# Before the attention, elementwise work of GpSimd moved to VectorE, with embedding preparation and inverse products queued elsewhere

## The chip, the cores and the metric

The kernel runs on one core of a Trainium2 chip. TensorE (PE) multiplies matrices, VectorE (DVE), ScalarE (ACT) and GpSimd (POOL) do elementwise work, SyncE (SP) starts most transfers. Each engine works through its own list of instructions in the order in which they were put there when the kernel was built; semaphores hold an instruction until its inputs are there. The metric is the device time of one execution, in microseconds; less is better.

## The reference, cut to what matters

One layer on 1024 tokens of width 1024, all in float32:

```
h    = layer_norm(x)
proj = h @ w_in                                   # 3600 columns
q,k,v = silu(causal_conv4(proj[:, :1536]))        # 4 delta-rule heads of 128
z     = proj[:, 1536:2048]
o_gdn = gated_delta_rule(q, k, v, beta, decay)    # by chunks: (I + A)^-1, then a scan over chunks
fq,fk,fv = proj[...]                              # 8 attention heads of 64
o_fox = rms_norm(forgetting_attention(fq, fk, fv))
h = layer_norm(ALPHA*h + concat(rms_norm(o_gdn)*silu(z), o_fox) @ w_out)
ff  = square(relu(h @ w_up)) @ w_down
ple = (p @ w_ple) * sigmoid(h @ w_ple_gate)
out = layer_norm(ALPHA*h + ff + ple)
```

## The kernel before, in words

Precision first: float32 operands of a big matmul are split into a rounded half (`_hi`, a ScalarE cast) and a remainder (`_lo`, the difference of the two, `split_lo`, L54), and three products are summed.

The work runs in stages.

1. **Start** (L226 to L330). `p` and `w_ple` are loaded; `ple_prep` (L275 to L278) transposes `p` on TensorE and splits it (`pth`, `ptl`); `ple_mm` (L286) makes 16 tiles of the embedding product and sends them to DRAM. The weights of the values, `wv`, are loaded in eight tiles and split. Then for each of the eight token tiles `ln_rows` normalises a row tile `h`, `to_act` transposes it into `act_hi`/`act_lo`, and 48 matmuls `psv` (L309) make the attention's values and the gates.
2. **Projections** (`proj_ch`, L216). A projection column is 128 outputs for all tokens: its weights are loaded and split by `load_w` (`in_raw`, `in_hi`, `in_lo`), then two halves of 24 matmuls fill one PSUM bank each, of three. `conv_silu` (tiles `g`, `cv`) follows for the 12 delta-rule columns; `fox_proj` (`fq`, `fk`) and `z_proj` (`gz`) make the 12 others.
3. **Delta-rule set work**, for a pair of heads at a time (`hp` 0 and 1). `gdn_a` makes the chunk matrices (`tm` decay, `qd`, `kd`, `ka`, `am`); `gdn_fs` inverts 32x32 blocks by 31 forward steps of two VectorE operations each (`ftmp`, `ft`), writes them to DRAM and reads them back as `tm` and `ttm`; `gdn_b` combines blocks to full inverses with matmuls (`ps_p`, `ps_tp`, `ps_ttp`); `gdn_chain` scans eight chunks (`ps_ks`, `ps_vn`, `ps_s`, `ps_o`).
4. **Attention** (`ps_sc`, `ps_pt`, `ps_av`), then the output projection (`ps_mix`), the MLP and the last norm. The diff leaves these as they are, but projections that are not done when the attention starts (`fq`, `fk`, `gz`) run between its matmuls; the last `gz` columns stand in one run in front of the last two attention heads.

The order on each engine is made when the kernel is built: a scheduler takes instructions by priority (`tc.cur_priority`, lower first) and by its own idea of when they are ready. `background` (L658) gives the `fq`, `fk` and `gz` columns a priority 20000 later than the rest, so that they fill TensorE where nothing else is ready. Nothing reorders the lists at run time.

## Time and profile before

| | |
|---|---|
| median of 3 runs | 1489.93 us (1484.91 to 1490.1) |
| the profiled execution | 1487.18 us, of which 1485.5 us from its first to its last instruction (the span) |
| busy time in the span | PE 1398.8, weight loads 1177.5, DVE 1084.3, ACT 561.6, POOL 249.4 us |
| instructions | 20635 |

All of POOL's busy time lies in the first 700 us, in which the stages 1 to 4 up to the output projection run. A busy PE means that at least one matmul was under way, by modelled ends; times of waits are those of the engine that stood idle, and the name behind an arrow is what ended the wait.

### The profile page before, as it was taken

Reading aid. Unit: us, or ns where it says so; the run is one execution under the profiler, and the core shown is the slowest. Engines: PE = TensorE matmul, PEld = TensorE weight load, DVE = VectorE, ACT = ScalarE, POOL = GpSimd, SP = SyncE. Lnnn points to the kernel's source line nnn. Section 1 sums busy time; section 2 is a strip of 40 time slices with the busy share of each in tenths; the row PEclk is TensorE's granted clock in tenths of the full one; section 3 lists DMA queues with packets and bytes.
Section 4 is the critical chain, followed back from the end, with each engine's and each line's share of the span. In section 5 each row is a group of like instructions: output and inputs, shape, how many; then the busy total and the mean of one; then the engine's idle time right before and its main releaser. Section 6 shows DMA issues by size and latency. Waiting matters only on the chain.

```text
span 1485.5 us, 20635 instructions
## 1 busy us (share of the span) xinstructions
PE 1398.8 (94%) x7342; PEld 1177.5 (79%) x7342; DVE 1084.3 (73%) x2222; ACT 561.6 (38%) x1024; POOL 249.4 (17%) x196
## 2 busy tenths in 40 slices
PE   4999999789899899989999999999999999999997
PEld 3888787777788787777888988888888888888885
DVE  6647799567567887274889877777777789657877
ACT  4432422232136676272113333333333444455431
POOL 4313351036106433442000000000000000000000
PEclk9999999999999999999999999999999999999999
DMA  6765432525534333523377674444444986334342
GB/s 222 254 187 170 158 100 78 160 84 161 149 107 140 99 97 95 160 86 114 135 240 221 184 245 148 154 150 148 147 141 147 327 299 211 98 99 126 109 140 80
DMA packets 196638, 229.11 MB, mean 154 GB/s; under 512 B 23877, under 2 KB 129590, under 8 KB 196534
## 3 DMA queue, kind: packets, MB, share of 16 engines
q1 hardware_dynamic: 187142, 221.48, 47.5%
q10 hardware_dynamic: 9008, 5.24, 1.4%
q8 instruction: 58, 0.95, 0.3%
q0 software_dynamic: 384, 1.06, 0.2%
q14 instruction: 46, 0.38, 0.1%
HBM read 152.14 MB, written 75.60 MB: 153 GB/s over the span
## 4 chain that ended last, share of the span: by engine, by line
PE 70%; DVE 14%; DMA 6%; issue 3%; ACT 2%; POOL 2%; SPq 0%; DVEq 0%; ACTq 0%; POOLq 0%
PE ps_uP L1186 21%; PE ps_da L1306 9%; PE ps_db L1306 9%; DVE cv L51 4%; PE ps_gP L1053 4%; PE ps_db L1412 3%; PE gz L216 3%; PE psv L309 3%; PE ps_mix L932 2%; PE ps_av L779 2%; DVE ft L48 2%; PE ps_pt L765 2%; DVE ftmp L48 2%; PE g L216 1%; PE fk L216 1%
## 5 line engine op out<-in xcount | busy, mean ns | idle before, releaser
L1186 PE MATMUL ps_uP<-T,uS 128*128 128x512 f32 x576 | 133.8, 390 | 0.0
L1186 PEld LDWEIGHTS ps_uP<-T,uS 128*128 128x128 f32 x576 | 108.1, 188 | 23.4
L1276 ACT CAST rh<-rr 128x512 fp32r<-128x512 f32 x112 | 69.8, 623 | 138.8 <-PE ps_da L1306 51.6
L54 DVE TENSOR_TENSOR rl<-rr,rh 128x512 fp32r<-128x512 f32 x112 | 76.9, 687 | 59.0 <-ACT rh L1276 24.8
L1186 PE MATMUL ps_uP<-B,uA 128*128 128x512 f32 x384 | 92.2, 395 | 0.0
L932 PE MATMUL ps_mix<-wo,act_hi 128*128 128x512 f32 x256 | 82.8, 398 | 3.8 <-POOL wo L54 1.7
L1186 PEld LDWEIGHTS ps_uP<-B,uA 128*128 128x128 f32 x384 | 72.0, 188 | 17.4
L216 PE MATMUL g<-act_hi,in_hi 128*128 128x512 f32 x192 | 75.9, 395 | 3.4 <-DVE cv L51 3.3
L54 POOL TENSOR_TENSOR in_lo<-in_raw,in_hi 128x1024 fp32r<-128x1024 f32 x24 | 58.9, 2454 | 114.9 <-ACT in_hi L190 114.9
L216 PE MATMUL g<-act_hi,in_lo 128*128 128x512 f32 x192 | 76.0, 396 | 0.0
L216 PE MATMUL g<-act_lo,in_hi 128*128 128x512 f32 x192 | 75.8, 395 | 0.0
L1276 ACT CAST rl<-B 128x512 fp32r<-128x512 f32 x96 | 59.6, 622 | 24.6 <-PE ps_db L1306 12.4
L1181 ACT CAST uS<-wS 128x512 fp32r<-128x512 f32 x64 | 39.5, 622 | 73.2 <-issue 48.2
L54 DVE TENSOR_TENSOR uA<-uraw,uA 128x512 fp32r<-128x512 f32 x48 | 33.1, 690 | 46.3 <-ACT uA L1181 46.3
L54 DVE TENSOR_TENSOR ql<-B,rl 128x512 fp32r<-128x512 f32 x96 | 65.6, 684 | 0.3
L51 DVE SCALAR_TENSOR_TENSOR cv<-g,hcw,cv 128x511 f32<-128x511 f32 (+2 forms) x72 | 53.2, 739 | 7.9 <-ACT cv L413 7.5
L932 PEld LDWEIGHTS ps_mix<-wo,act_hi 128*128 128x128 f32 x256 | 47.5, 189 | 14.3 <-POOL wo L54 2.4
L54 DVE TENSOR_TENSOR ptl<-ps_pt,pth 128x512 fp32r<-128x512 f32 (+2 forms) x96 | 51.0, 552 | 9.3 <-ACT pth L767 8.9
L743 ACT ACTIVATE s<-s,m 128x128 f32<-128x128 f32 (+3 forms) x64 | 49.9, 780 | 13.0 <-DVE m L740 12.7
L765 PE MATMUL ps_pt<-ident,s 128*128 128x128 f32 x288 | 45.6, 275 | 9.0 <-DVE szl L51 4.0
L767 ACT CAST pth<-ps_pt 128x512 fp32r<-128x512 f32 (+2 forms) x96 | 43.9, 477 | 19.9 <-PE ps_pt L765 18.6
L1306 PE MATMUL ps_db<-rl,rh 128*128 128x512 f32 x192 | 51.3, 389 | 0.0
(372 smaller groups left out, 3836.3 us busy)
## 6 DMA issues: line engine op xcount, KB each, us to landing
uraw<-in_w_up_dram SPq DMA_DIRECT2D x32, 512.0 KB, 4.5
B<-in_w_down_dram SPq DMA_DIRECT2D x32, 512.0 KB, 5.5
rr<-rS SPq DMA_DIRECT2D x64, 256.0 KB, 2.7
in_raw<-in_w_in_dram SPq DMA_DIRECT2D x24, 512.0 KB, 3.8
rr<-rA SPq DMA_DIRECT2D x48, 256.0 KB, 2.9
h_spill<-h SPq DMA_DIRECT2D x16, 512.0 KB, 4.0
qkr<-qk_spill SPq DMA_DIRECT2D x32, 256.0 KB, 4.2
rA<-ub SPq DMA_DIRECT2D x32, 256.0 KB, 2.2
```

What stands on the lines that cost most here:

```text
L48: eng.tensor_tensor(out=o, in0=a, in1=b, op=op)
L51: nc.vector.scalar_tensor_tensor(out=o, in0=a, scalar=s, in1=b, op0=op0, op1=op1)
L54: eng.tensor_tensor(out=lo, in0=src, in1=hi.bitcast(F32), op=ALU.subtract)
L216: nc.tensor.matmul(ps, w[:, k, :], a[n][:, :, k], start=(k == 0 and wi == 0), stop=(k == NK - 1 and wi == 2))
L309: nc.tensor.matmul(ps[:, 0:264], a[t // 4][:, t % 4, k], w[:, k, _sl(n, 264)], start=(k == 0 and wi == 0), stop=(k == NK - 1 and wi == 2))
L743: nc.scalar.activation(out=s[:, :W], in_=s[:, :W], func=AF.Exp, bias=m[:, i:i + 1], scale=-1.0, accum_out=pairs[h // 2][2][:, r, j:j + 1])
L765: nc.tensor.transpose(pt[:, i], s[:, _sl(k0 + i)], ident)
L932: nc.tensor.matmul(ps, a[t // 4][:, t % 4, k], w, start=(k == 0 and wi == 0), stop=(k == NK - 1 and wi == 2))
L1053: nc.tensor.matmul(ps[j // 2][:, j % 2], B[b][s][k][:, _sl(j)], a[w][:, k], start=(first and j % 2 == 0 and k == 0 and wi == 0), stop=(j % ...
L1186: nc.tensor.matmul(ps[p], w[:, k], B[t][b][k], start=(chain is None and k == 0 and wi == 0), stop=(k == 3 and wi == 2), skip_group_check=c ...
L1276: nc.scalar.copy(out=hi, in_=src)
L1306: nc.tensor.matmul(ps[j], rs[x][:, _sl(j)], qs[y], start=(not chain and c == 0 and wi == 0), stop=(c == NP - 1 and wi == 2), skip_group_ch ...
```

## The change

It has four parts.

- Tensor operations that stood on GpSimd now stand on VectorE: the remainders of `load_w` and of `wv` (24 of 128x1024 and 8 of 128x520), the four operations per pair on `tm`, the two each on `qd`, `am`, `ka`, `kd`, and half of the last product on `vb`. `ln_rows` of the first norm takes its VectorE form: one product of a subtraction for the whole row and one product with a sum for each half, in place of a ScalarE, a VectorE and a GpSimd operation.
- The embedding's rows are taken in another order (`(q t)` for `(t q)`), so that a partition reads four whole rows in one piece. The first `ple_prep` stands ahead of the small VectorE work of the start, the second one ahead of the second column half of the first four tiles.
- `issue_after(x)` puts a block's instructions behind instruction `x` on x's engine; it adds no wait. `gdn_b(0)` goes behind the first half of column `fq0` on TensorE, `gdn_b(1)` behind the first half of `fk2`, and the exponential of the second pair's `tm` behind the end of the first chain on ScalarE.
- Priorities: the remaining delta-rule columns 2000, the background 20000, the second pair 4000 later.

```diff
@@ load_w, load_wv
-        split_lo(nc.gpsimd, wl, raw, wh)
+        split_lo(nc.vector, wl, raw, wh)
...
-                split_lo(nc.gpsimd, wv_lo[:, k, 0:520], raw, wv_hi[:, k, 0:520])
+                split_lo(nc.vector, wv_lo[:, k, 0:520], raw, wv_hi[:, k, 0:520])
@@ start
-        pv = p.rearrange("(t q) c -> q t c", q=P)
+        pv = p.rearrange("(q t) c -> q t c", t=NT)
+        ple_rows = ple_spill.rearrange("(q t) c -> t q c", t=NT)
...
-            nc.sync.dma_start(out=ple_spill[_sl(t), _sl(n, 512)], in_=so)
-        for half in range(2):
-            ple_prep(half)
-            for n in range(2):
-                for t in range(half * 4, half * 4 + 4):
-                    ple_mm(t, n)
+            nc.sync.dma_start(out=ple_rows[t, :, _sl(n, 512)], in_=so)
+        prep0 = ple_prep(0)
+        with tc.issue_after(prep0):
+            nc.vector.tensor_copy(out=wv_hi[:, :, 520:528], in_=wvs)
+            split_lo(nc.vector, wv_lo[:, :, 520:528], wvs, wv_hi[:, :, 520:528])
+        for t in range(4):
+            ple_mm(t, 0)
+        ple_prep(1)
+        for t in range(4):
+            ple_mm(t, 1)
+        for n in range(2):
+            for t in range(4, 8):
+                ple_mm(t, n)
...
-            ln_rows(xts.pop(t), gb, bb, h, "spread")
+            with tc.issue_after(prep0) if t == 0 else ExitStack():
+                ln_rows(xts.pop(t), gb, bb, h)
@@ gdn_a
-            tt(nc.gpsimd, c["tm"], c["tm"], gam[:, h * 8:h * 8 + 8].unsqueeze(2).to_broadcast([P, 8, P]), ALU.subtract)
-            tt(nc.gpsimd, c["tm"], c["tm"], mask_d.unsqueeze(1).to_broadcast([P, 8, P]), ALU.add)
-            nc.scalar.activation(out=c["tm"], in_=c["tm"], func=AF.Exp)
-            tt(nc.gpsimd, c["qd"], c["ka"][:, 1], c["am"], ALU.mult)
+            tt(nc.vector, c["tm"], c["tm"], gam[:, h * 8:h * 8 + 8].unsqueeze(2).to_broadcast([P, 8, P]), ALU.subtract)
+            tt(nc.vector, c["tm"], c["tm"], mask_d.unsqueeze(1).to_broadcast([P, 8, P]), ALU.add)
+            with tc.issue_after(chain_end[0]) if hp else ExitStack():
+                nc.scalar.activation(out=c["tm"], in_=c["tm"], func=AF.Exp)
+            tt(nc.vector, c["qd"], c["ka"][:, 1], c["am"], ALU.mult)
...
-            tt(nc.gpsimd, c["am"], c["ka"][:, 1], m32.unsqueeze(1).to_broadcast([P, 8, P]), ALU.mult)
+            tt(nc.vector, c["am"], c["ka"][:, 1], m32.unsqueeze(1).to_broadcast([P, 8, P]), ALU.mult)
...
-            tt(nc.gpsimd, c["ka"][:, 1], c["ka"][:, 1], m64.unsqueeze(1).to_broadcast([P, 8, P]), ALU.mult)
-            tt(nc.gpsimd, c["kd"], c["kd"], cc[:, 1, 8 * j:8 * j + 8].unsqueeze(2).to_broadcast([P, 8, P]), ALU.mult)
+            tt(nc.vector, c["ka"][:, 1], c["ka"][:, 1], m64.unsqueeze(1).to_broadcast([P, 8, P]), ALU.mult)
+            tt(nc.vector, c["kd"], c["kd"], cc[:, 1, 8 * j:8 * j + 8].unsqueeze(2).to_broadcast([P, 8, P]), ALU.mult)
@@ end of gdn_chain
-                tt(nc.vector if half else nc.gpsimd, vb[:, cs], vb[:, cs],
+                tt(nc.vector, vb[:, cs], vb[:, cs],
@@ end of the set work
-    gdn_b(0)
-    gdn_chain(0)
-    gdn_proj(2)
-    gdn_proj(3)
-    background((fox_proj, 0), (fox_proj, 1), (fox_proj, 2), (fox_proj, 3), *((z_proj, h) for h in range(GH)))
-    gdn_a(1)
-    gdn_fs(1)
-    gdn_b(1)
+    now = tc.cur_priority
+    tc.cur_priority = now + 2000
+    gdn_proj(2)
+    gdn_proj(3)
+    tc.cur_priority = now + 20000
+    for pr in range(4):
+        fox_proj(pr)
+    for h in range(GH):
+        z_proj(h)
+    tc.cur_priority = now
+    with tc.issue_after(last_mm["fq0", 0]):
+        gdn_b(0)
+    gdn_chain(0)
+    tc.cur_priority = now + 4000
+    gdn_a(1)
+    gdn_fs(1)
+    with tc.issue_after(last_mm["fk2", 0]):
+        gdn_b(1)
     gdn_chain(1)
```

What this makes of the order shows in three places. The first is VectorE's list from its first work on (`x_131` is the first token tile, `w_lo_ple` the remainder of the embedding's weights, `wvr` the raw tiles of `wv`); before:

```order
L54 TENSOR_TENSOR w_lo_ple_126<-w_raw_ple_124,w_hi_ple_125 128x1024
L85 CAST identb<-ident 128x128
L140 BN_STATS st<-x_131 128x6 x2
L54 TENSOR_TENSOR pT_lo<-ps_pT,pT_hi 128x512
L252 CAST wv_hi<-wv_s 128x8x8
L54 TENSOR_TENSOR pT_lo<-ps_pT,pT_hi 128x512
```

and of the change:

```order
L54 TENSOR_TENSOR w_lo_ple_126<-w_raw_ple_124,w_hi_ple_125 128x1024
L85 CAST identb<-ident 128x128
L280 TENSOR_TENSOR pT_lo<-ps_pT,pT_hi 128x512 x2
L295 CAST wv_hi<-wv_s 128x8x8
L140 BN_STATS st<-x_131 128x6
L54 TENSOR_TENSOR w_lo_ple_135<-w_raw_ple_133,w_hi_ple_134 128x1024
L54 TENSOR_TENSOR wv_lo<-wvr_143,wv_hi 128x520
L54 TENSOR_TENSOR wv_lo<-wvr_147,wv_hi 128x520
```

The embedding's remainders `pT_lo` moved ahead of the statistics of the first token tile, and the remainders of `wv` came onto this list.

The second place is VectorE's list behind the 16 products `ka` of the first pair, up to the first forward step; before, the `vb` products were followed by ten convolution products and the `ftmp` step, and the six operations on `am`, `kd` and `ka` stood on GpSimd:

```order
L48 TENSOR_TENSOR kd_1706<-kd_1706,cc_1802 128x1024
L48 TENSOR_TENSOR kd_1720<-kd_1720,cc_1802 128x1024
L48 TENSOR_TENSOR am_1701<-ka_1704,m_1225 128x1024
L48 TENSOR_TENSOR am_1703<-ka_1718,m_1225 128x1024
L48 TENSOR_TENSOR ka_1704<-ka_1704,m_1226 128x1024
L48 TENSOR_TENSOR ka_1718<-ka_1718,m_1226 128x1024
```

Of the change, on VectorE:

```order
L48 TENSOR_TENSOR am_1693<-ka_1696,m_1217 128x1024
L48 TENSOR_TENSOR am_1695<-ka_1710,m_1217 128x1024
L48 TENSOR_TENSOR kd_1698<-kd_1698,cc_1794 128x1024
L48 TENSOR_TENSOR ka_1696<-ka_1696,m_1218 128x1024
L48 TENSOR_TENSOR ka_1710<-ka_1710,m_1218 128x1024
L48 TENSOR_TENSOR kd_1712<-kd_1712,cc_1794 128x1024
```

The six operations stand one behind the other in front of the four products on `vb` and of the forward steps; the ten convolution products now stand among the steps.

The third place is TensorE's list where `gdn_b(0)` begins (`ps_p`); the last projection column of the delta rule is `g_2804` before and `g_2427` in the change. Before:

```order
L216 MATMUL g_2804<-act_lo_84,in_hi 128x512
L585 MATMUL ps_p<-tm_1700,am_1701 128x128 x4
L216 MATMUL g_2804<-act_hi_83,in_lo 128x512
L216 MATMUL g_2804<-act_hi_83,in_hi 128x512
L216 MATMUL g_2804<-act_lo_84,in_hi 128x512
L585 MATMUL ps_p<-tm_1702,am_1703 128x128 x4
```

Of the change, the end of the 24 matmuls of `fq` and what follows:

```order
L218 MATMUL fq_2470<-act_hi_81,in_hi 128x512
L218 MATMUL fq_2470<-act_lo_82,in_hi 128x512
L218 MATMUL fq_2470<-act_hi_81,in_lo 128x512
L597 MATMUL ps_p<-tm_1692,am_1693 128x128 x4
L597 MATMUL ps_p<-tm_1694,am_1695 128x128 x4
```

Ahead of the first `ps_p` stand 569 matmuls `g` before, and 576 `g` and 24 `fq` in the change. Up to the first matmul of the attention TensorE has 281 matmuls `fq` and `fk` before and 346 in the change; the run of `gz` in front of the last two heads has 145 before and 56 in the change.

## Rows read from the trace of the kernel before

**Rows 1.** The page's busy times: us, share of the span, instructions.

```profile
PE 1398.8 (94%) x7342; PEld 1177.5 (79%) x7342; DVE 1084.3 (73%) x2222; ACT 561.6 (38%) x1024; POOL 249.4 (17%) x196
```

**Rows 2.** Waits of TensorE in 0 to 622 us: total, times, longest.

```profile
PE ps_p L585 <- DMA tm<-img: 12.6, 2, 8.3
PE ps_ple L286 <- ACT pT_hi L277: 8.0, 2, 6.0
...
PE ps_ple L286 <- DVE pT_lo L54: 4.9, 1, 4.9
PE ps_vn L618 <- ACT vb L638: 4.5, 1, 4.5
...
PE g L216 <- DVE cv L51: 3.3, 2, 2.0
...
PE ps_tr L167 <- POOL h L48: 2.5, 1, 2.5
PE ps_kt L505 <- DMA ka<-conv_spill: 2.4, 2, 2.3
...
PE ps_aq L530 <- DVE ka L51: 2.3, 1, 2.3
PE psv L309 <- DVE ve L51: 1.5, 1, 1.5
```

**Rows 3.** Stretches: length, busy PE, PEld, DVE, ACT, POOL (instructions), PEclk, DMA share, GB/s.

```profile
0.00:45.00 45.00, 26.00 (x91) 19.47 (x91) 27.26 (x55) 18.64 (x30) 20.46 (x26) 0.92 0.69 223
...
218.50:266.00 47.50, 44.11 (x192) 35.62 (x192) 46.58 (x106) 13.57 (x20) 9.67 (x4) 1.00 0.28 88
...
589.00:622.00 33.00, 32.76 (x145) 26.76 (x143) 9.48 (x27) 8.34 (x14) 12.51 (x6) 1.00 0.48 146
sum 622.00, PE 560.42 PEld 476.10 DVE 434.83 ACT 244.05 POOL 217.71; mean PE 46.70 PEld 39.68 DVE 36.24 ACT 20.34 POOL 18.14
```

**Rows 4.** The seven stretches of clock 0.5 before the attention: first, last, sum.

```profile
36.60:43.40 6.80, 6.21 (x15) 4.85 (x16) 3.96 (x16) 3.19 (x7) 2.39 (x1) 0.50 0.68 222
...
398.40:405.20 6.80, 6.04 (x25) 5.78 (x26) 0.00 (x0) 2.29 (x4) 2.35 (x1) 0.50 1.15 312
sum 34.10, PE 28.75 PEld 25.14 DVE 16.26 ACT 10.24 POOL 11.74; mean PE 4.11 PEld 3.59 DVE 2.32 ACT 1.46 POOL 1.68
```

**Rows 5.** VectorE in order of time, 29.9 to 34.5 us: start, duration.

```profile
32.83 1.20 DVE L51 SCALAR_TENSOR_TENSOR nwb<-ve,nwt 128x1 f32<-128x1 f32 x1
34.06 0.16 DVE L51 SCALAR_TENSOR_TENSOR ve<-nwb,ve 128x1 f32<-128x1 f32 x1
```

**Rows 6.** VectorE in order of time, 223.5 to 229 us.

```profile
224.21 0.31 DVE L48 TENSOR_TENSOR ftmp<-fa,ft 64x156 f32<-64x156 f32 x1
224.56 2.39 DVE L48 TENSOR_TENSOR ft<-ft,ftmp 64x156 f32<-64x156 f32 x1
```

**Rows 7.** GpSimd in order of time, 200 to 275 us.

```profile
204.48 4.79 POOL L48 TENSOR_TENSOR am<-ka,m 128x1024 f32<-128x1024 f32 x2 [1.71 <-DVE ka L51]
209.50 4.77 POOL L48 TENSOR_TENSOR ka<-ka,m 128x1024 f32<-128x1024 f32 x2 [0.23 <-DMA img<-ka]
...
224.27 2.51 POOL L54 TENSOR_TENSOR in_lo<-in_raw,in_hi 128x1024 fp32r<-128x1024 f32 x1 [7.20 <-ACT in_hi L190]
```

**Rows 8.** GpSimd by group up to 455 us: busy us, mean ns, idle before.

```profile
L54 POOL TENSOR_TENSOR in_lo<-in_raw,in_hi 128x1024 fp32r<-128x1024 f32 x20 | 48.3, 2417 | 109.2 <-ACT in_hi L190 109.2
L48 POOL TENSOR_TENSOR h<-h,bb 128x1024 f32<-128x1024 f32 x8 | 19.1, 2386 | 41.9 <-PE psv L309 20.9 <-DVE h L48 13.5 <-issue 4.6
```

**Rows 9.** VectorE by group up to 455 us, same columns.

```profile
L51 DVE SCALAR_TENSOR_TENSOR cv<-g,hcw,cv 128x511 f32<-128x511 f32 x24 | 17.8, 741 | 7.5 <-ACT cv L413 7.5
...
L51 DVE SCALAR_TENSOR_TENSOR ve<-nwb,ve 128x1 f32<-128x1 f32 x24 | 11.7, 487 | 0.6
...
L48 DVE TENSOR_TENSOR h<-h,gb 128x1024 f32<-128x1024 f32 x8 | 9.8, 1222 | 3.1 <-ACT h L158 3.0
...
L48 DVE TENSOR_TENSOR vb<-ps_vt,cc 128x512 f32<-128x512 f32 x8 | 5.1, 682 | 0.3 <-PE ps_vt L549 0.2
```

**Rows 10.** The chain that ended last, 260 to 335 us: start, us, what.

```profile
266.09 3.46 DMA img<-ft
...
269.56 5.77 DMA tm<-img
...
306.18 2.31 POOL tm L48
```

More of the change, by code (lines that the diff above doesn't have):

```diff
@@ L207, in proj_w @@
         return load_w(w_in[:, col:col + P], f"in{col}")
+    last_mm = {}
     def proj_ch(col, name):
@@ L215, in proj_ch @@
                 for wi, (w, a) in enumerate(((wh, act_hi), (wh, act_lo), (wl, act_hi))):
-                    nc.tensor.matmul(ps, w[:, k, :], a[n][:, :, k],
-                                     start=(k == 0 and wi == 0), stop=(k == NK - 1 and wi == 2))
+                    mm = nc.tensor.matmul(ps, w[:, k, :], a[n][:, :, k],
+                                          start=(k == 0 and wi == 0), stop=(k == NK - 1 and wi == 2))
+            last_mm[name, n] = mm.ins
             yield n, ps
@@ L251, in tile_block @@
         nc.sync.dma_start(out=wvs, in_=w_in[:, 2048:2056].rearrange("(k q) c -> q k c", q=P))
-        nc.vector.tensor_copy(out=wv_hi[:, :, 520:528], in_=wvs)
-        split_lo(nc.vector, wv_lo[:, :, 520:528], wvs, wv_hi[:, :, 520:528])
         def load_wv(k0):
@@ L277, in ple_prep @@
                 nc.scalar.copy(out=hi, in_=ps)
-                split_lo(nc.vector, ptl[:, k, _sl(half, 512)], ps, hi)
+                lo = nc.vector.tensor_tensor(out=ptl[:, k, _sl(half, 512)], in0=ps, in1=hi.bitcast(F32), op=ALU.subtract)
+            return lo.ins
         def ple_mm(t, n):
@@ L600, in gdn_b @@
                     tt(nc.vector, ttm[:, cs], ttm[:, cs], ps2, ALU.subtract)
+    chain_end = {}
     def gdn_chain(hp):
@@ L637, in gdn_chain @@
                 nc.tensor.matmul(ps[:, 0:P], c["ka"][:, 2, ch], vn[h], start=(ch == 0), stop=True)
-                nc.scalar.activation(out=c["vb"][:, ch], in_=ps[:, 0:P], func=AF.Copy, scale=c["rq"][:, ch:ch + 1])
+                chain_end[hp] = nc.scalar.activation(out=c["vb"][:, ch], in_=ps[:, 0:P], func=AF.Copy,
+                                                     scale=c["rq"][:, ch:ch + 1]).ins
         ss = gr.tile([P, 2, 8], F32, tag="sso", name=f"sso{hp}", bufs=1)
@@ L653, in gdn_chain @@
                 cs = slice(half * 4, half * 4 + 4)
-                tt(nc.vector if half else nc.gpsimd, vb[:, cs], vb[:, cs],
+                tt(nc.vector, vb[:, cs], vb[:, cs],
                    ro[:, 8 * j + half * 4:8 * j + half * 4 + 4].unsqueeze(2).to_broadcast([P, 4, P]), ALU.mult)
             nc.sync.dma_start(out=o_spill[h], in_=vb.rearrange("q c i -> q (c i)"))
-    def background(*fns):
-        now = tc.cur_priority
-        tc.cur_priority = now + 20000
-        for f, i in fns:
-            f(i)
-        tc.cur_priority = now
     gdn_proj(0)
```

## The prediction

> **What bounds the kernel now.** I read the page's busy times first: TensorE is busy in 94% of the span, VectorE in 73%, GpSimd in 17% [rows 1]. So the end is set by TensorE's work plus its idle time. The diff leaves TensorE's matmuls as they are; it can only change when TensorE waits and at which clock it runs. Hence the second view, TensorE's waits up to 622 us, where the last run of projection columns ends: PE is busy for 560.4 of these 622 us [rows 3], which leaves 61.6 us. The list [rows 2] says where: 12.6 us at the two starts of `gdn_b` for `tm` read back from DRAM, 8.0 and 4.9 us in the embedding product for `pT_hi` and `pT_lo`, 4.5 us in the first scan, 3.3 us for convolution products, 2.5 and 1.5 us in the first norm, 2.4 us at the transposes `ps_kt`, and 2.3 us at `ps_aq`. The third view is the granted clock: before the attention seven stretches, 34.1 us together, run at 0.50, which is the 1.2 GHz level [rows 4]; each begins during or soon after one of the waits. Work done there takes twice as long, so they cost up to 17 us on top.
>
> What is saved in front of the attention must reach the end. It does so through the run of `gz` matmuls: 145 in 33 us, PE busy throughout, 0.228 us each [rows 3]. This is background work that did not fit earlier. A matmul done earlier in a gap shortens that run, and behind the run nothing is changed. The order shows the same in counts: 65 more background matmuls ahead of the attention, 14.8 us, and 89 fewer in the run.
>
> **GpSimd and VectorE stand in each other's way.** At 224.56 us a forward step of 64x156 takes 2.39 us; the one before it, same size, took 0.31 [rows 6]. At 224.27 GpSimd had begun a remainder that took 2.51 us [rows 7]: the step ends when GpSimd ends. The same at the start: a VectorE operation on 128x1 takes 1.20 us while GpSimd works, 0.16 when it doesn't [rows 5]; the group's mean is 487 ns [rows 9], so its 24 instructions lose about 24 x 0.33 = 8 us. Convolution products, which read PSUM and one tensor of SBUF, keep their 741 ns throughout [rows 9]. So a GpSimd operation that meets a two-tensor VectorE operation costs VectorE about 2 us. The same 128x1024 operation on VectorE takes 1.22 us against 2.42 [rows 8, 9]. The move therefore costs VectorE little or nothing in total, and takes a wait of 2 us out of chains of small operations.
>
> The Trainium skill says why (SBUF — State Buffer, "SBUF: two separate sides"): the two engines share one pair of ports as an exclusive lock for the whole instruction, and the other blocks. The trace agrees: 2.39 us against 2.51. The skill also has a rule against this change (Perfetto Trace Analysis, "Optimizing Scalar/DVE Operations"): a saturated VectorE may be relieved by moving work to another engine, even GpSimd, with the caution that the shared port may undo it. By its first half the sum would be that of the second rival below.
>
> **The change part by part.** Its own time is that of the profiled execution, 1487.2 us (0.2% under the median of 1489.9).
>
> *Start.* Now `pT_lo` stands behind statistics of a token tile still being loaded (the wait of 4.9 us), and the second `pT_hi` comes late (6.0), followed by 6.8 us at half clock worth 3.4 [rows 2, 4]. In the change the remainder stands first and the small operations are no longer stretched. That is 14 us, not all won: ScalarE still evacuates the first product behind casts of weights that are being loaded, and three PSUM banks are full by then; and the first `psv` needs a normalised tile. For that VectorE has, once the first token tile is there at about 14 us (it is idle-free from there), eight `wv` remainders of 0.7 us, some six statistics of 0.7, one 1.2 us remainder twice, two norms at 1.2 + 2 x 0.7, and some 40 small operations of 0.16: about 26 us, so 40 us instead of 45. I take 5; bounds 0 and 12.
>
> *Norms.* The eight tiles lose GpSimd's 2.39 us and a ScalarE step from their latency; VectorE gets about 1.4 us more per tile. The waits of 2.5 and 1.5 us and a stretch of 3.4 us at half clock hang on this. I take 4.5 of 5.7; bounds 0 and 6.
>
> *Transposes.* The 2.4 us at `ps_kt` wait for convolution, store and load; one stretch less on that path. I take 1; bounds -1 and 4.
>
> *First inverse.* Here VectorE is full: 46.6 of 47.5 us [rows 3]. The change puts six 1.22 us operations ahead of the steps. Before, GpSimd began `am` at 204.5 and `ka` at 209.5, when the image had been stored [rows 7]. On VectorE: `am`, `am`, `kd` to 208.9, wait to 209.5, three more to 213.2, four `vb` of 0.68 [rows 9] to 215.9, when the steps begin: 2.6 us earlier than at 218.5. The steps' stretch has 120 rows instead of 104: seven convolution products more (7 x 0.74 = 5.2), five remainders more (6.1), four collisions less (4 x 2.1 = 8.4): 2.9 us longer. So the steps end at the same time, and so do store and load, 3.5 and 5.8 us [rows 10]. But TensorE now has 31 more matmuls to do until then, 7.1 us, in the wait of 8.3. With half of the 6.8 us stretch after it gone (1.7) I take 8.5; bounds 0 (the steps end 8.5 us later) and 13 (the stalls on `cv` go too).
>
> *First scan.* ScalarE's exponential of `tm` waited for GpSimd, and the scan's evacuations stood behind it: `tm` on GpSimd lies in the chain until 308.5 [rows 10], 4.5 us idle, then 3.4 us at half clock. The exponential now goes behind the scan; ScalarE has nothing to do there while the next pair is loaded. The four `tm` operations, 4.9 us, now stand between VectorE's copies in the scan, and TensorE gets more `fq` matmuls there. I take 4.5; bounds 1 and 7.
>
> *Second pair.* At `ps_aq` 2.3 us and half of 3.4 hang on VectorE, which gets two `qd` (2.4 us) and two `vb` more and loses a collision; TensorE gets ten more matmuls (2.3 us) ahead of the last `ps_aq`. I take 3; bounds 0 and 4. The second inverse begins about 2 us later by the same six operations, and is shorter by four collisions less three remainders (8.4 - 3.7); TensorE gets 14 more matmuls (3.2 us). Together that covers its wait of 4.3 us, and most of 6.8 us at half clock. I take 6.5; bounds 2 and 8.
>
> *New waits.* Remainders now stand in VectorE's list between other work: in front of copies that TensorE waits for, about 20 times 1.2 us before the attention. Where VectorE has slack (before the steps it is busy for under 80%) that is hidden; I take off 5 us; bounds 0 and 12.
>
> Edits I cost at nothing: the embedding's row order (the same bytes in larger pieces, and the first load lies at the start, where TensorE waits for it anyway; up to 1 us either way), and the remainders during the attention, which replace GpSimd work that collides there.
>
> Sum: 5 + 4.5 + 1 + 8.5 + 4.5 + 3 + 6.5 - 5 = 28 us. 1487.2 - 28 = **1459 us**.
>
> **The rivals.**
>
> *Given back behind the attention's start.* The run of `gz` falls from 33 to 12.7 us, and under it the output weights and the last heads are prepared (GpSimd busy for 12.5 us of it, ScalarE 8.3 [rows 3]). If the attention needs that time anyway, up to 20 of the 28 us return: 1479. Against it: both are idle for most of the run, and the loads hang on buffers of the columns, which come free earlier as well.
>
> *VectorE becomes the bound in the set work.* The inverse's steps end as much later as they got work: the six operations and five remainders, 13 us, without the 8.4. Then the terms of both inverses and `ps_aq` fall to 0 and the scan's to 1; start and norms remain: 1487 - (5 + 4.5 + 1 + 1) + 5 = 1480. For it: 98% busy there. Against it: the collisions seen.
>
> *Slower: a remainder blocks VectorE's list.* On GpSimd, `in_lo` sat waiting for ScalarE's cast (109 us of idle time before 20 of them [rows 8]), which harms nobody there. In VectorE's list the same wait holds the steps behind it; the cast itself waits for TensorE to finish with the column two before. Eight remainders stand inside the two inverses; at 3.5 us each they eat the 28 us, and at 6 us, half a column's 48 matmuls (10.9 us), the time is 1507. Against it: in the order each stands behind the convolution products of the column that frees its buffer, so that the cast should be done.
>
> **How the numbers follow.** My forecast 0.70, given back 0.09, VectorE the bound 0.14, blocked 0.07. The forecast's own range, from its bounds taken partly together, is 1446 to 1473; to leave out no more than 2 in 10 I go to 1477 on the upper side. About 0.5%, 7.4 us, is what can be told from no change here: faster means under 1482. Faster has the forecast and most of the first two rivals: 0.90. Same 0.05, slower 0.05.
>
> **What would show it.** GpSimd's busy time up to 455 us falls to a few us, and no VectorE operation on 128x1 takes over 0.3 us. TensorE's wait for `pT_lo` is gone, its first `psv` begins near 40 us. The waits at `ps_p` fall from 12.6 to under 4 us together, `ps_vn` on ScalarE is gone, and the stretches at half clock before the attention fall from 34 us to under 15. The run of 56 `gz` matmuls ends near 594 us. I am wrong if the steps of the first inverse take over 52 us, or if waits for `in_lo` show up on VectorE, or if TensorE's waits between the run's end and 700 us grow.

## The result, and the profile after

The changed kernel takes 1448.9 us (median of 4 runs, 1447.75 to 1451.71) against 1489.86 in the same job: 0.9739 of the time before, 95% interval 0.9719 to 0.976. The prediction was 1459, in a range of 1445 to 1477. The profiled execution took 1447.75 us, 39.4 less than that of before.

The page's busy times, to be held against [rows 1]:

```profile
PE 1387.1 (96%) x7342; PEld 1167.7 (81%) x7342; DVE 1091.0 (75%) x2290; ACT 553.1 (38%) x1016; POOL 102.6 (7%) x128
```

VectorE has 68 instructions more and is busy only 6.7 us longer, while GpSimd lost 146.8 us: the moved operations take half the time there, and those that GpSimd stretched are short again. TensorE has the same 7342 matmuls and is busy 11.7 us less, as fewer of them ran at half clock (the 0.50 in PEclk).

TensorE's waits up to 578 us, where the last run of projection columns now ends (total, times, longest), against [rows 2]:

```profile
PE ps_pT L277 <- DMA p_raw<-in_p_dram: 5.2, 1, 5.2
PE g L218 <- DVE edge L431: 5.0, 1, 5.0
...
PE ps_tp L606 <- DMA ttm<-img: 2.8, 2, 1.6
```

`ps_p`, `pT_lo`, `ps_vn` and `ps_aq` are gone from the list, and a wait for `edge` is new. Behind the run one has grown, the wait for `szl`, over 560 to 760 us:

```profile
PE ps_pt L783 <- DVE szl L51: 8.9, 1, 8.9
```

Before, over 560 to 790 us:

```profile
PE ps_pt L765 <- DVE szl L51: 4.0, 2, 2.9
```

Where the time came from is read by stage. The stretches below have the same first and last work in both kernels: up to the first `psv`; to the last `psv`; to the first forward step; to the first `ps_vn`; to the second pair's first step; to the first `ps_sc`; to the end of the run of `gz`; to the last `ps_mix`. The columns are those of [rows 3]. Before:

```profile
0.00:51.50 51.50, 32.50 (x120) 24.74 (x121) 28.70 (x58) 22.02 (x35) 22.86 (x27) 0.93 0.71 230
51.50:114.70 63.20, 58.01 (x447) 55.24 (x446) 36.21 (x99) 21.11 (x38) 14.42 (x7) 0.97 0.69 202
114.70:218.60 103.90, 99.72 (x458) 82.23 (x457) 85.82 (x169) 33.99 (x56) 47.39 (x22) 0.98 0.48 146
218.60:296.00 77.40, 65.67 (x360) 56.37 (x358) 61.17 (x129) 20.09 (x31) 10.79 (x6) 0.96 0.41 121
296.00:360.70 64.70, 57.03 (x330) 48.77 (x329) 44.12 (x116) 20.03 (x42) 32.96 (x16) 0.95 0.40 128
360.70:447.80 87.10, 81.20 (x494) 72.21 (x493) 55.60 (x123) 21.17 (x41) 14.60 (x8) 0.96 0.45 121
447.80:621.80 174.00, 166.29 (x1011) 136.53 (x1009) 123.20 (x333) 105.44 (x243) 74.69 (x85) 1.00 0.40 118
621.80:767.90 146.10, 134.47 (x711) 109.93 (x712) 102.97 (x261) 51.14 (x102) 31.66 (x28) 0.99 0.39 128
```

After:

```profile
0.00:39.10 39.10, 29.86 (x122) 22.81 (x122) 24.65 (x67) 20.24 (x35) 4.60 (x16) 1.00 0.91 305
39.10:97.00 57.90, 55.64 (x442) 53.82 (x443) 37.65 (x107) 13.71 (x30) 0.08 (x1) 1.00 0.75 219
97.00:193.90 96.90, 94.36 (x443) 78.36 (x442) 80.93 (x176) 34.61 (x56) 1.01 (x2) 1.00 0.50 153
193.90:273.90 80.00, 75.63 (x401) 64.71 (x402) 65.97 (x153) 22.72 (x35) 1.10 (x2) 0.96 0.48 134
273.90:335.90 62.00, 61.25 (x364) 52.22 (x363) 52.52 (x125) 21.07 (x42) 0.00 (x0) 1.00 0.43 137
335.90:419.30 83.40, 79.82 (x499) 70.02 (x497) 53.02 (x129) 21.42 (x41) 3.51 (x3) 1.00 0.48 133
419.30:578.00 158.70, 151.43 (x946) 124.00 (x945) 126.74 (x338) 101.89 (x238) 57.76 (x77) 1.00 0.38 112
578.00:729.10 151.10, 135.04 (x711) 110.02 (x712) 103.54 (x261) 51.44 (x102) 34.55 (x30) 0.97 0.40 131
```

Length less busy PE is TensorE's idle time. Half of the busy time at 0.50 comes on top: a matmul of 128x512 begins every 0.43 us there and every 0.23 us otherwise. Idle time inside such a stretch is counted among the waits already, so that the seven stretches of [rows 4], with 28.75 us of busy PE, cost 14.4 us and not the prediction's upper bound of 17. Besides the first and the last of [rows 4], these ran at 0.50 before, up to the last `ps_mix` (first and last us, then as above):

```profile
98.00:101.40 3.40, 3.18 (x13) 2.47 (x13) 2.04 (x4) 2.30 (x3) 0.61 (x1) 0.50 0.94 211
186.80:190.20 3.40, 3.40 (x15) 3.00 (x14) 3.40 (x4) 0.00 (x0) 3.29 (x2) 0.50 0.00 0
272.10:278.90 6.80, 3.43 (x13) 3.17 (x14) 1.86 (x4) 1.21 (x2) 0.00 (x0) 0.50 1.19 304
309.60:313.10 3.50, 3.23 (x15) 3.23 (x16) 1.58 (x4) 1.26 (x4) 0.00 (x0) 0.51 0.19 71
347.20:350.60 3.40, 3.26 (x8) 2.63 (x9) 3.40 (x10) 0.00 (x0) 3.09 (x2) 0.50 0.00 0
627.10:630.50 3.40, 3.40 (x16) 3.02 (x15) 2.11 (x4) 1.76 (x5) 1.20 (x3) 0.50 0.97 340
```

In the changed kernel two are left there, one begun during the wait for `edge`, the other during that for `szl`:

```profile
195.10:202.00 6.90, 4.52 (x11) 3.59 (x12) 6.89 (x22) 1.26 (x2) 0.00 (x0) 0.51 0.10 38
580.80:591.10 10.30, 4.11 (x15) 3.34 (x16) 3.37 (x9) 3.55 (x8) 5.04 (x4) 0.50 0.65 205
```

| stretch, up to | lost before, idle + half clock | lost after | gain, us | term predicted |
|---|---|---|---|---|
| first `psv` | 19.0 + 3.1 | 9.2 | 12.9 | 5 |
| last `psv` (norms) | 5.2 + 1.6 | 2.3 | 4.5 | 4.5 |
| first forward step | 4.2 + 1.7 | 2.5 | 3.3 | 1 |
| first `ps_vn` (first inverse) | 11.7 + 1.7 | 4.4 + 2.3 | 6.8 | 8.5 |
| second pair's first step | 7.7 + 3.2 | 0.7 | 10.2 | 4.5 + 3 |
| first `ps_sc` (second inverse) | 5.9 + 3.0 | 3.6 | 5.3 | 6.5 |
| end of the run of `gz` | 7.7 | 7.3 | 0.4 | 0 |
| last `ps_mix` | 11.6 + 1.7 | 16.1 + 2.1 | -4.8 | 0 (a rival) |

The gains, taken before rounding, sum to 38.7 us, and the last `ps_mix` comes 38.8 us earlier (729.1 against 767.9); 0.7 us more come behind it. In the row of the first inverse the new wait for `edge`, 5.0 and 2.3 us, is taken off already; the prediction had such waits in a term of their own, -5.

### The profile page after: what moved, and what is told of

Its sections match the earlier page's. It is cut to its first block, busy times and chain, and to the rows that moved or that the text cites. A ratio compares the mean times of both kernels' runs of the same rounds, so it can differ in the third digit from the quotient of the medians.

```text
span 1446.0 us, 20592 instructions
## 1 busy us (share of the span) xinstructions
PE 1387.1 (96%) x7342; PEld 1167.7 (81%) x7342; DVE 1091.0 (75%) x2290; ACT 553.1 (38%) x1016; POOL 102.6 (7%) x128
## 4 chain that ended last, share of the span: by engine, by line
PE 78%; DVE 9%; DMA 7%; issue 3%; ACT 2%; POOL 1%; SPq 0%; DVEq 0%; ACTq 0%; POOLq 0%
PE ps_uP L1204 21%; PE ps_da L1324 9%; PE ps_db L1324 9%; PE g L218 6%; PE ps_gP L1071 5%; PE ps_db L1430 3%; PE fk L218 3%; PE ps_mix L950 3%; PE psv L320 3%; PE ps_av L797 2%; PE fq L218 2%; PE gz L218 2%; PE ps_pt L783 2%; DVE h L51 2%; DVE cv L51 1%
## 5 line engine op out<-in xcount | busy, mean ns | idle before, releaser
L1294 ACT CAST rh<-rr 128x512 fp32r<-128x512 f32 x112 | 69.8, 623 | 141.5 <-PE ps_db L1324 47.9
L1199 ACT CAST uS<-wS 128x512 fp32r<-128x512 f32 x64 | 39.4, 621 | 73.2 <-issue 48.2
L950 PEld LDWEIGHTS ps_mix<-wo,act_hi 128*128 128x128 f32 x256 | 47.5, 188 | 14.1 <-POOL wo L54 2.4
L783 PE MATMUL ps_pt<-ident,s 128*128 128x128 f32 x288 | 45.3, 277 | 14.1 <-DVE szl L51 8.9
L51 DVE SCALAR_TENSOR_TENSOR cv<-g,hcw,cv 128x510 f32<-128x510 f32 (+2 forms) x72 | 53.4, 741 | 1.0 <-ACT cv L424 0.5
L1324 PE MATMUL ps_db<-ql,rh 128*128 128x512 f32 x192 | 51.3, 389 | 0.0
L1324 PE MATMUL ps_db<-rl 128*128 128x512 f32 x192 | 51.3, 389 | 0.0
```

The source lines that it names most:

```text
L51: nc.vector.scalar_tensor_tensor(out=o, in0=a, scalar=s, in1=b, op0=op0, op1=op1)
L783: nc.tensor.transpose(pt[:, i], s[:, _sl(k0 + i)], ident)
L950: nc.tensor.matmul(ps, a[t // 4][:, t % 4, k], w, start=(k == 0 and wi == 0), stop=(k == NK - 1 and wi == 2))
L1294: nc.scalar.copy(out=hi, in_=src)
L1324: nc.tensor.matmul(ps[j], rs[x][:, _sl(j)], qs[y], start=(not chain and c == 0 and wi == 0), stop=(c == NP - 1 and wi == 2), skip_group_ch ...
```

## The experiments

Times are medians, and the ratio is to the kernel before on the same chip, with its 95% interval. The question was first which half of the change wins, then what the waits for `edge` and `szl` cost.

**The moves alone.** All tensor operations on VectorE, nothing else:

```diff
-        split_lo(nc.gpsimd, wl, raw, wh)
+        split_lo(nc.vector, wl, raw, wh)
...
-            ln_rows(xts.pop(t), gb, bb, h, "spread")
+            ln_rows(xts.pop(t), gb, bb, h)
...
-            tt(nc.gpsimd, c["am"], c["ka"][:, 1], m32.unsqueeze(1).to_broadcast([P, 8, P]), ALU.mult)
+            tt(nc.vector, c["am"], c["ka"][:, 1], m32.unsqueeze(1).to_broadcast([P, 8, P]), ALU.mult)
```

> The kernel before with the tensor operations alone moved from GpSimd to VectorE (column and value-weight remainders, the products of the set work, the first norm's form, half of the last product); the embedding and every priority and queue place as before. Theory (both halves of the change win, about equally): the stretched small operations of the start and the wait for GpSimd at the transposes and at the exponential of tm go, the two waits at ps_p stay at 10 us or more since nothing new is queued ahead of them: 1470, between 1462 and 1477. Rival, the order does it all: VectorE takes over what GpSimd did and wins nothing, 1485 or more. Rival, the moves do it all: 1452 or less.

Measured: 1460.44, ratio 0.9818 (0.9796 to 0.9839), 27.7 us less. TensorE's waits up to the end of its run of `gz`, 593.3 us:

```profile
PE ps_ple L286 <- DVE pT_lo L54: 7.0, 1, 7.0
PE g L216 <- DVE edge L420: 5.1, 1, 5.1
...
PE ps_p L585 <- DMA tm<-img: 4.0, 2, 2.4
```

More than expected, and in a place that was not expected: the waits at `ps_p` fell from 12.6 to 4.0 us, though nothing was put ahead of them by hand. The order that is built for this kernel is another one, however. From the first forward step to the first `ps_p` its trace has 222 matmuls, where the kernel before has 194; the 28 more are 6.4 us at 0.228 us each, and this one wait fell from 8.3 to 1.6 us. So matmuls ahead of `ps_p` cover the wait here too, and the moves alone are not free of a change of order. The wait for `pT_lo` grew from 4.9 to 7.0, and the one for `edge` is there already, so that it comes with the moves.

**The order alone.** The changed kernel with every moved operation back on GpSimd:

```diff
-        split_lo(nc.vector, wl, raw, wh)
+        split_lo(nc.gpsimd, wl, raw, wh)
...
-                ln_rows(xts.pop(t), gb, bb, h)
+                ln_rows(xts.pop(t), gb, bb, h, "spread")
...
-            tt(nc.vector, c["am"], c["ka"][:, 1], m32.unsqueeze(1).to_broadcast([P, 8, P]), ALU.mult)
+            tt(nc.gpsimd, c["am"], c["ka"][:, 1], m32.unsqueeze(1).to_broadcast([P, 8, P]), ALU.mult)
```

> The changed kernel with every moved tensor operation put back on GpSimd (the first norm in its old form too); the embedding's order, the priorities and the places behind fq0, fk2 and the first chain stay. Theory: the waits at ps_p are covered by the fq and fk matmuls, under 4 us together, but VectorE's small operations are stretched again to 2 us where GpSimd works: 1470, between 1462 and 1478. Rival, the order does it all: 1452 or less. Rival, the moves do it all: 1485 or more.

Measured: 1478.87, ratio 0.994 (0.9921 to 0.9959), 9.2 us less. The same view, up to 615 us:

```profile
PE ps_p L597 <- DMA tm<-img: 7.2, 2, 5.9
```

The time lies just above the expected range. Here 7.2 us stay at `ps_p` in spite of the places behind `fq0` and `fk2`, 5.9 of them at the second pair. The two halves together, 36.9 us, are near the 41 of the whole; three quarters are the moves.

**The start alone**, on the kernel before (the diff of the change's start, with the remainders of `wv` and the first norm on VectorE):

```diff
+        prep0 = ple_prep(0)
...
-                split_lo(nc.gpsimd, wv_lo[:, k, 0:520], raw, wv_hi[:, k, 0:520])
+                split_lo(nc.vector, wv_lo[:, k, 0:520], raw, wv_hi[:, k, 0:520])
```

> The kernel before with only the start of the changed kernel: the embedding's rows and order, the value-weight remainders and the first norm on VectorE; column remainders, set work, priorities and places as before. The changed kernel ends its last psv 17.7 us earlier than before (97.0 against 114.7). Theory: a matmul done earlier shortens the run of gz in front of the last heads, so all of that reaches the end: 1473, between 1469 and 1478, with a run of about 70 gz matmuls fewer or the columns done that much earlier. Rival, the later stages wait for something else and give it back: 1483 or more.

Measured: 1469.48, ratio 0.9872 (0.985 to 0.9895), 18.6 us less. The stretch up to its last `psv`, columns as in [rows 3]:

```profile
0.00:98.10 98.10, 86.15 (x564) 76.97 (x565) 61.23 (x172) 34.03 (x64) 7.05 (x18) 1.00 0.81 251
```

It comes there 16.6 us earlier (98.1 against 114.7), and all of that reaches the end. The run of `gz` still has its 145 matmuls and ends at 605.9 instead of 621.8: everything behind the start is simply earlier. Its first `psv` begins at 39.0 us, as in the changed kernel (39.1); with the moves alone it begins at 44.4 and with the order alone at 46.6, against 51.5 before, so that both halves are needed there. What the embedding's other row order does by itself was not tried.

**The column remainders back on GpSimd**, 24 operations of the changed kernel:

```diff
-        split_lo(nc.vector, wl, raw, wh)
+        split_lo(nc.gpsimd, wl, raw, wh)
```

> The changed kernel with the 24 column remainders alone back on GpSimd (2.4 us each there, 1.22 on VectorE). Theory: some of them meet forward steps and set products, which then take 2 us longer each; VectorE's time saved is lost again: 1455, between 1450 and 1462. Rival, VectorE is the bound of the set work in the changed kernel, so that 24 operations fewer help it: 1444 or less. Rival, both cancel: within 2 us of the changed kernel, 1447 to 1451.

Measured: 1459.94, ratio 0.9814 (0.9797 to 0.9831): 11 us of the gain are gone. The first pair's forward steps on VectorE, with the shortest, middle and longest duration in ns, and the first and last start:

```profile
L48 DVE TENSOR_TENSOR ft<-ft,ftmp x31: 182/346/2467, 202.0 to 248.6; 64x31 f32<-64x31 f32 x2, 64x60 f32<-64x60 f32 x2, 64x87 f32<-64x87 f32 x2, 64x112 f32<-64x112 f32 x2
```

In the changed kernel the longest takes 411 ns. The longest one here, in VectorE's list (start, duration), and GpSimd's operation at the same time:

```profile
213.36 2.47 DVE L48 TENSOR_TENSOR ft<-ft,ftmp 64x220 f32<-64x220 f32 x1
```

```profile
213.00 2.58 POOL L54 TENSOR_TENSOR in_lo<-in_raw,in_hi 128x1024 fp32r<-128x1024 f32 x1 [16.29 <-ACT in_hi L190]
```

TensorE's waits up to 594.6 us:

```profile
PE ps_p L597 <- DMA tm<-img: 8.7, 1, 8.7
PE g L218 <- DVE edge L431: 6.0, 1, 6.0
```

The 8.7 us stand at the second pair, where the changed kernel has none: its steps begin 8.7 us later (344.6 against 335.9) and take 28.6 us instead of 26.1. The delays add up on the way there; how much of them is stretched operations and how much the place in GpSimd's list was not taken apart.

**Without the two places behind `fq0` and `fk2`:**

```diff
-    with tc.issue_after(last_mm["fq0", 0]):
-        gdn_b(0)
+    gdn_b(0)
...
-    with tc.issue_after(last_mm["fk2", 0]):
-        gdn_b(1)
+    gdn_b(1)
```

> The changed kernel without the two places behind fq0 and fk2: both gdn_b go where the scheduler puts them; priorities and everything else stay. Theory: TensorE stands before ps_p until tm is back from DRAM, in the first pair and in the second, as in the kernel with the moves alone (4.0 us and 2.2 us there) or in the kernel before (12.6): 1455, between 1451 and 1460. Rival, the priorities alone put enough fq and fk matmuls ahead: 1447 to 1451.

Measured: 1453.73, ratio 0.9764 (0.9728 to 0.9799), 4.8 us over the changed kernel by the medians, though the two intervals overlap. In TensorE's waits up to 585 us the one for `tm` is back:

```profile
PE ps_p L597 <- DMA tm<-img: 5.3, 3, 2.2
```

and 6.8 us at 0.50 (373.5 to 380.3 us) with it.

**The wait for `szl`.** SyncE's list in the changed kernel shows why it is 8.9 us long (start, duration):

```profile
573.98 1.06 SPq L458 DMA_DIRECT2D z_spill<-sz  x2
581.05 0.32 SPq L851 DMA_DIRECT2D o<-o_spill  x1
581.47 0.86 SPq L854 DMA_DIRECT2D szl<-z_spill  x2
```

The first head's gates were stored long before (the stores of its two halves were issued at 451.1 and 483.7 us), but their load stands behind stores of later gates, whose buffers it shares, and behind the load of `o`, which waits 3.5 us for GpSimd's `kl`. The edit takes other buffers, which are free by then:

```diff
-            s = cp.tile([P, 512], F32, tag="cv", name="szl", bufs=3)
+            s = cp.tile([P, 512], F32, tag="th", name="szl", bufs=3)
```

> The changed kernel with one tag changed: the tiles szl (the gates z read back for the output of the delta-rule heads) take the free buffers of the convolution's th instead of those that sz is written to, so that their loads need not stand behind the last stores of sz and the load of o. Theory (part of the change's gain is given back behind the run of gz: TensorE waits 8.9 us for szl and then has 10.2 us at half clock, some 5 us): 1435, between 1431 and 1440, with no wait of TensorE for szl over 2 us. Rival, the last heads need that time for their own keys (load, cast and remainder on GpSimd) and wait there instead: 1446 or more.

Measured: 1443.67, ratio 0.9694 (0.9665 to 0.9724). Its slowest run, 1445.25, is below the changed kernel's fastest, 1447.75, though the two ratio intervals just touch. The wait is gone, the stretch at half clock fell from 10.2 to 3.4 us and the longest run of `gz` to 26 matmuls. But 5.2 us came of it, not 14, and the time lies between the expected range and the rival's. Of the 10.2 us at half clock TensorE was busy for 4.1, which cost 2.1 us and not 5, so that 11 us were the most to be won. From the first `ps_sc` to the last `ps_mix` it takes 303.0 us against 309.8; of these 6.8 us, 2.2 are lost again up to the MLP (94.7 against 92.5). Over 560 to 760 us TensorE's longest wait is now one that took 0.2 us in the changed kernel:

```profile
PE ps_mix L950 <- POOL act_lo L54: 2.5, 2, 2.3
```

**The wait for `edge`.** VectorE's list of the changed kernel shows it:

```profile
190.40 1.22 DVE L48 TENSOR_TENSOR kd<-kd,cc 128x1024 f32<-128x1024 f32 x1
191.53 2.48 DVE L48 TENSOR_TENSOR vb<-ps_vt,cc 128x512 f32<-128x512 f32 x4
193.93 0.18 DVE L48 TENSOR_TENSOR ftmp<-fa,ft 64x31 f32<-64x31 f32 x1
194.02 0.74 DVE L51 SCALAR_TENSOR_TENSOR cv<-g,hcw,cv 128x511 f32<-128x511 f32 x1
...
197.18 0.15 DVE L431 COPY edge<-g 128x3 f32<-128x3 f32 x1
```

The column whose products begin at 194.0 has been ready for them since its first step on ScalarE, which began at 187.8 and took 0.68 us; six products of the set work and four `vb` stand ahead. TensorE has no PSUM bank free and stops from 192.5 to 197.5. Four edits try this place. First a later priority for `ka`, `kd` and `vb`:

```diff
+        if hp == 0:
+            tc.cur_priority += 2200
         for j, h in enumerate(hs):
             c = H[h]
             tt(nc.vector, c["ka"][:, 1], c["ka"][:, 1], m64.unsqueeze(1).to_broadcast([P, 8, P]), ALU.mult)
...
+        if hp == 0:
+            tc.cur_priority -= 2200
```

> The changed kernel with ten operations of the first pair's set work (ka, kd and the evacuations vb) given a priority 2200 later, so that the convolution products of the column that is just then finished stand ahead of them and they come to stand between forward steps. Theory (the six operations put in front of the steps hold up the convolution, TensorE waits 5.0 us for the edge copy and then has 6.8 us at half clock, 3.4 us): 1441, between 1438 and 1445. Rival, VectorE is full there, the steps end that much later and the wait moves to ps_p: 1447 or more.

Measured: 1453.36, ratio 0.9758 (0.973 to 0.9786). In TensorE's waits from 100 to 420 us the one for `edge` is gone, and the next column's products are waited for longer:

```profile
PE g L218 <- DVE cv L51: 9.7, 1, 9.7
```

With this wait goes a longer stretch at 0.50 than the changed kernel's 6.9 us:

```profile
203.70:217.40 13.70, 7.20 (x16) 5.25 (x17) 13.43 (x32) 0.63 (x1) 0.00 (x0) 0.50 0.33 97
```

The steps end at 242.8 (242.1 in the changed kernel). The time is the rival's, but the wait moved to the convolution and not to `ps_p`; by the intervals it is not told apart from the changed kernel. VectorE is full there, busy for 13.4 of these 13.7 us, so that what is put later holds up somebody else.

**Both edits** (`szl` and the priority).

```diff
+            tc.cur_priority += 2200
...
+            s = cp.tile([P, 512], F32, tag="th", name="szl", bufs=3)
```

> Both: the tag of szl and the later priority of ka, kd and vb in the first pair. Theory: two separate waits, the gains add up: 1427, between 1421 and 1434. Rival, a matmul won ahead of the attention no longer reaches the end once the run of gz is spread over the last heads: within 3 us of the kernel with the tag alone.

Measured: 1445.95, ratio 0.9711 (0.9681 to 0.9741), not told apart from the tag alone. It lies within the rival's 3 us, but decides nothing about the sum, since one of its parts won nothing.

**`kd` and `vb` on ScalarE:**

```diff
-            tt(nc.vector, c["kd"], c["kd"], cc[:, 1, 8 * j:8 * j + 8].unsqueeze(2).to_broadcast([P, 8, P]), ALU.mult)
+            for ch in range(8):
+                nc.scalar.activation(out=c["kd"][:, ch], in_=c["kd"][:, ch], func=AF.Copy, scale=cc[:, 1, 8 * j + ch:8 * j + ch + 1])
...
+                for i in range(4):
+                    nc.scalar.activation(out=c["vb"][:, half * 4 + i], in_=ps[:, i], func=AF.Copy,
+                                         scale=cc[:, 2, 8 * j + half * 4 + i:8 * j + half * 4 + i + 1])
```

> The changed kernel with kd (scaled in place) and the evacuations vb of both pairs on ScalarE, in pieces of 128x128 with a scale per row, instead of VectorE: 32 small operations a pair there, some 10 us by the 364 ns of a like evacuation, and 5 us of VectorE's time a pair less. Theory (VectorE is full ahead of and in the inverses, ScalarE is not; what leaves VectorE in front of the steps lets the convolution products come earlier): the wait of 5.0 us for the edge copy and the 6.8 us at half clock behind it go: 1441, between 1437 and 1445. Rival, ScalarE's list holds up the first convolution step and the cast of the next column: 1449 or more.

Measured: 1447.19, ratio 0.972 (0.9689 to 0.9752): outside the expected range, and not told apart from the changed kernel. The wait for `edge` is gone, and no stretch at 0.50 is left before 536 us. But TensorE then waits at the inverses (its waits from 100 to 420 us):

```profile
PE ps_tp L608 <- DMA ttm<-img: 3.9, 3, 1.7
PE ps_p L599 <- DMA tm<-img: 2.5, 3, 1.1
...
PE g L218 <- DVE edge L431: 0.2, 1, 0.2
```

In the changed kernel these were 2.8 and 0. The steps end at 243.0 (242.1 in the changed kernel), and VectorE is busy for 47.2 of their 47.9 us.

**`kd` on GpSimd, and `kd` alone on ScalarE:**

```diff
-            tt(nc.vector, c["kd"], c["kd"], cc[:, 1, 8 * j:8 * j + 8].unsqueeze(2).to_broadcast([P, 8, P]), ALU.mult)
+            tt(nc.gpsimd, c["kd"], c["kd"], cc[:, 1, 8 * j:8 * j + 8].unsqueeze(2).to_broadcast([P, 8, P]), ALU.mult)
```

> The changed kernel with only the four products on kd back on GpSimd (2.4 us each there). Theory (GpSimd holds up VectorE only where VectorE reads two tensors of SBUF): kd can go as soon as its scale is there, while VectorE evacuates the products ka out of PSUM, which GpSimd doesn't stretch; so VectorE wins 2.4 us a pair as with kd on ScalarE, and part of the wait of 5.0 us goes: 1445, between 1442 and 1448. Rival, every operation on GpSimd costs VectorE its length there: am and ka are stretched to 2.4 us: 1450 or more.

> The changed kernel with only the products on kd on ScalarE, in 16 pieces of 128x128 a pair; the evacuations vb stay on VectorE. Theory: half of what kd and vb together bring: 1445, between 1442 and 1448. Rival, ScalarE holds up the first convolution step: 1449 or more.

Measured: 1449.15, ratio 0.9735 (0.9702 to 0.9768), and 1446.1, ratio 0.9719 (0.9691 to 0.9747). Neither is told apart from the changed kernel; the first lies outside the range expected of it. With `kd` on GpSimd, GpSimd and VectorE in order of time show that it costs VectorE nothing:

```profile
176.98 3.75 POOL L48 TENSOR_TENSOR kd<-kd,cc 128x1024 f32<-128x1024 f32 x2 [79.21 <-DVE cc L48]
```

```profile
176.75 6.35 DVE L51 SCALAR_TENSOR_TENSOR ka<-ps_aq,cc,tm 128x256 f32<-128x256 f32 x16
183.02 2.35 DVE L48 TENSOR_TENSOR am<-ka,m 128x1024 f32<-128x1024 f32 x2
```

In the changed kernel, with nothing on GpSimd, the same products take:

```profile
177.07 6.36 DVE L51 SCALAR_TENSOR_TENSOR ka<-ps_aq,cc,tm 128x256 f32<-128x256 f32 x16
```

So the products out of PSUM, 0.4 us each, are not held up by the two operations of 1.9 us on GpSimd that run beside the first of them, and the two `am` behind them take 1.2 us each. The mechanism was right, the gain was not there: the wait for `edge` fell to 3.9 us, and 6.9 us at 0.50 still followed.

**`szl` in other buffers and `kd` on ScalarE**, the best of both places:

```diff
-            tt(nc.vector, c["kd"], c["kd"], cc[:, 1, 8 * j:8 * j + 8].unsqueeze(2).to_broadcast([P, 8, P]), ALU.mult)
+            for ch in range(8):
+                nc.scalar.activation(out=c["kd"][:, ch], in_=c["kd"][:, ch], func=AF.Copy, scale=cc[:, 1, 8 * j + ch:8 * j + ch + 1])
...
-            s = cp.tile([P, 512], F32, tag="cv", name="szl", bufs=3)
+            s = cp.tile([P, 512], F32, tag="th", name="szl", bufs=3)
```

> The changed kernel with two edits that each won a little by themselves: szl in the free buffers of th (1443.7 alone, 5.2 under the changed kernel) and the products on kd in pieces on ScalarE (1446.1 alone, 2.8 under it). Theory (two waits in different stages, the one between 190 and 200 us, the other behind the last gz matmuls): the gains add up, 1441, between 1438 and 1443, and faster than both kernels of the study. Rival, what is won ahead of the attention is lost again in the last heads, where the gz matmuls are now spread: 1444 or more.

Measured over five rounds: 1438.69 (1437.11 to 1439.92), ratio 0.9671 (0.9658 to 0.9684). It is faster than both kernels, by 48 and some 10 us. That the gains add is not shown: the medians of the two alone, 5.2 and 2.8 us, make 8, but neither `kd` by itself nor this kernel against the tag alone is told apart by the intervals. The wait for `edge` is still 4.0 us here.

## Why the prediction was right, point by point

**Faster, by the moves off GpSimd: shown.** The moves alone won 27.7 us, and 24 operations put back cost 11. No `nwb` or `ve` on 128x1 takes over 0.23 us now (203 to 221 and 104 to 163 ns), against 1.20 in [rows 5]; in the inverse's steps GpSimd does nothing. How much of the gain is the end of this stretching is not shown: a moved operation is also shorter in itself (1.22 us against 2.4), and the order built around it is another. The first half of the rule that the prediction weighed (the Trainium skill, Perfetto Trace Analysis, "Optimizing Scalar/DVE Operations": a saturated VectorE may hand work even to GpSimd) does not hold for the remainders here, and its caution does. What decides is what VectorE reads meanwhile: a step that reads two tensors of SBUF took 2.47 us beside a remainder, where none takes over 0.42 without GpSimd, and sixteen products out of PSUM took 6.35 us beside `kd` and 6.36 without. By the Trainium skill (SBUF — State Buffer, "SBUF: two separate sides") VectorE needs the ports that it shares with GpSimd when it has two inputs from SBUF and the GpSimd operation reads SBUF too. The trace agrees with both sides of that.

**The term that was off most is the start**, 5 us, which measured 12.9. The working was "so 40 us instead of 45". The 40 came near, the first `psv` begins at 39.1, though the items listed for it add up to 23.8 us and not to about 26. The 45 was wrong: in [rows 3] it is only where a stretch was cut. Before the change the embedding product still ran at 45 us, and the first `psv` began at 51.5, where the first stretch of before shown above ends. What the prediction held back for, ScalarE's evacuations (`ple_o`), cost TensorE 2.2 us, against 1.2 before. The start by itself brought 18.6 us with the norms, where 9.5 were predicted.

**The norms** (4.5, measured 4.5) and **the second inverse** (6.5, 5.3) came near what was worked out. **The first inverse** (8.5, 6.8) did so for partly other reasons: the wait at `ps_p` vanished as said, the steps took 48.2 us (50.4 were worked out), but the six operations in front of them held up the convolution by 5.0 us and 2.3 of half clock. That is the price the prediction had under new waits, 5 us over 20 places; it was 7.3 in one place, and not at a remainder. Without it the row would stand at 14.1, above the term's upper bound of 13, so that two misses cancel in part. **The scan and the second pair** brought 10.2 where 7.5 stood, and **the transposes** 3.3 where 1 stood; no run takes these apart.

**What covers `ps_p`.** The prediction gave it to the matmuls queued ahead, and the runs agree. The moves alone already leave 28 more of them between the first forward step and `ps_p`, by the order as built, and took 12.6 us down to 4.0. Without the two places 5.3 us of waits come back, 4.3 of them at the second pair; the time of some 5 us that this costs is within the noise.

**Given back behind the attention's start**: a rival with 9 in 100 and up to 20 us. It took place in part, 4.8 us, by a mechanism that it did not name: TensorE's waits for the output weights are the same in both kernels (1.7 us for GpSimd's part), and what grew, from 4.0 to 8.9 us, is the wait for one load of gates behind others in SyncE's list. It hid behind the larger gains ahead.

**VectorE as the bound of the set work**: not at 1480, but it is what stops the next step. It is busy for 98% of the steps (47.3 of 48.2 us), and the four edits that took work away in front of them, or put it later, left the end of the steps where it was, within 1 us (241.2 to 243.0, against 242.1).

**A remainder blocking VectorE's list**: waits for `in_lo` did show up on VectorE, 9.0 us over 21, and TensorE lost 0.6 us to them. Within the first pair's steps VectorE lost 0.4 us to them; the longest, 3.5 us, stands behind the second pair's.

**The run of 56 `gz`** ended at 578.0 instead of 594, by what the stages ahead brought beyond their terms. The prediction had the gains arrive by a shorter run. The start alone shows that they arrive without that too.

**The signs.** Most came as said: the waits at `ps_p` are gone, and 6.9 us at half clock are left ahead of the attention, of 34.1. GpSimd's busy time up to 455 us fell from 148.1 to 24.9 us and not to a few, as the attention, with work of its own for GpSimd, now begins at 419.3; up to there it is 10.3. Of the three signs of being wrong two did show, the waits for `in_lo` on VectorE and the longer waits behind the run; both were small against the gains. That the time lies in the range owes something to luck: the start, the scan with the second pair and the transposes brought 12.9 us more than their terms, and what was given back, nothing in the sum, took 4.8 of it.

## What to carry to other kernels

Where two elementwise engines block each other, count the operations of each that read two tensors of SBUF while the other works: here such a pair took as long as the longer of both (2.47 against 2.58 us), and products that read PSUM lost nothing. Before a term is sized, find the row of the instruction that the term is to move, in the kernel before too. A gain that shortens the work in front of a late stage can lengthen the waits for that stage's loads; the transfer queue's list there tells what has to be moved first.

## What was not expected of the hardware

Behind waits of TensorE for `edge` at nearly the same place the clock went differently: 3.9 us (`kd` on GpSimd) were followed by 6.9 us at 0.50, 4.0 us (the last kernel) by 3.4, and 2.9 us (`kd` on ScalarE) by none. What tells these apart is not shown, and the first and the last of the three differ by only 3 us in the medians, within their intervals.
